# Seven products in all three feed-forward stages, state-space parameters split over two of them, and streamed half tiles at odd multiples of 64 bytes

## The chip, the cores and the metric

The kernel runs on one core of a Trainium2 chip. A core has TensorE (PE in the rows, with its weight loads as PEld), VectorE (DVE), ScalarE (ACT), GpSimd (POOL), and SyncE (SP), which here issues all the DMAs. The metric is the device time of one execution in microseconds, less is better.

## The reference

Two layers of a first block, then one layer of a second block, on 512 tokens of width 1024, all in float32:

```python
# hybrid_layer, twice
h = rms_norm(x, g_mix_pre); u = h @ w_in
# band attention, a causal convolution and a retention on slices of u
mix = concatenate([y_att, y_conv, y_ret]) @ w_out
x = x + rms_norm(mix, g_mix_post)
h = rms_norm(x, g_mlp_pre)
f = square(relu(h @ w_up)) @ w_down            # 1024 -> 4096 -> 1024
x = x + rms_norm(f, g_mlp_post)

# second_block, once
proj = rmsnorm(h, norm1_gain) @ w_in           # q, k, v, u, gates
# differential attention on q, k, v
# s5_layer on u: lambda = exp((a_re + i a_im) * exp(log_dt)), a scan over time with it
h = h + (g_attn * attn_branch + g_ssm * ssm_branch) @ w_out
up = causal_dwconv(rmsnorm(h, norm2_gain) @ w_up)
gate, val = split(up)                          # 2816 each
h = h + (silu(gate) * val) @ w_down
```

The state-space part needs powers of lambda and tables of its cosines and sines. They depend on parameters alone, not on x.

## The kernel before

**Products.** Each float32 operand is split in two fp32r tiles, `hi` (rounded, by ACT's cast) and `lo` (the rest, by a subtraction), and each product is made as hi·hi + hi·lo + lo·hi: three matmuls (`mm3`). Weights stream in from HBM as `wraw` tiles of 128x1024 and are split to `whi`/`wlo` by class `Stream`. Normalized activations lie transposed in `hhi`/`hlo` (128 x 8 x 512). In a row's name the streamed (moving) operand comes first, then the stationary one: `ps<-hhi,whi` streams `hhi` against weights `whi`; `ps<-whi,fhi` streams weights against the activations `fhi`.

**Stages, in order.** Hybrid layer 0, its MLP (called MLP 0 here, rows from 261.9 us), hybrid layer 1, its MLP (MLP 1, from 888.6 us), the second block's mixer, and its feed-forward (FF 2, from 1742.4 us). An MLP has a head (`f_split`: four 128-wide chunks of `w_up`, done in two halves of 256 tokens), a body (the other 28 chunks and seven of eight groups of `w_down`) and a tail (the last group of `w_down`, the norms, and the transposes `to_hT` for what comes next).

**Seven products.** `FAST = (1,)` names the layers whose MLP takes two chunks of `w_up` at a time with seven products in place of eight (Strassen's scheme in Winograd's form): `take_fast` (line 808) makes sums of weight tiles (`wsum`), `fast_in` (1135) makes sums of activations (`sraw`, then `shi`/`slo`), and `FastUp` runs 7 x 4 x 3 = 84 matmuls of 256 columns for two chunks, with `mid` and `cu` as intermediates. Without it, two chunks are 2 x 8 x 3 = 48 matmuls of 512 columns. MLP 1 (`mlp`, 1708) has 14 such pairs and FF 2 (`ffn2`) has 20. MLP 0 (`mlp_plain`, 1649) has none.

**State-space parameters.** `ssm_params` (1802) is a side task of MLP 0. It makes small 128x32 values (`prm`) on DVE and ACT, eight `combine` results on POOL (`t<-sbc,prm`), and eight pairs of tables on POOL (`t<-t,prm` and `t<-t`, 42 operations a pair), each closed by one DVE multiply (`t<-t,pv`) and two DMAs. Each `yield 3000` puts the due time of what follows 3000 ns later.

**Order.** The program records all instructions (`Trace`) and a list scheduler gives them their order from due times and estimated costs, and an engine where two can do it: `sub` and `sum` go to DVE or POOL by a bias, chosen by `self.wbias` (3 favours POOL, 1 excludes it; 3 in `mlp_plain`, 1 in `mlp` and `ffn2`, 2 in the hybrid layers). Each engine then runs its queue in that order. An instruction may stand up to 25.16 us ahead of its due time. SBUF tiles of 128x512 come from one pool, `sp`, with 58 places.

**Addresses.** In the program before, every fp32r operand that is streamed through TensorE starts at a multiple of 256 bytes in its partition.

Of the kernel before, what the change touches and what calls it, by code (L numbers as in the profile page):

```python
# [17 lines left out]
P = 128  # L18
S = 512
# [27 lines left out]
NF2 = DFF2 // 128  # L47
FAST = (1,)

# [887 lines left out]
class Builder:  # L937
# [11 lines left out]
    def __init__(self, tc, ctx, A, out):  # L949
        self.tc, self.nc, self.A, self.out = tc, Trace(tc.nc), A, out  # L950

        def pool(name, bufs, shape=None, dtype=F32, space="SB"):
            kw = {} if space == "SB" else {"space": bass.MemoryType.PSUM if space == "PS" else bass.MemoryType.DRAM}
            return Pool(lambda n: ctx.enter_context(tc.tile_pool(name=n, bufs=1, **kw)), name, bufs, shape, dtype, space)
        self.cp = pool("cp", None)
        self.wr = pool("wr", self.NR, [P, 1024])
        self.wh, self.wl = pool("wh", self.NW, [P, 1024], F32R), pool("wl", self.NW, [P, 1024], F32R)
        self.sp = pool("sp", 86 - 2 * self.NR - 4 * self.NW, [P, 512])
        self.stp = pool("stp", 16, [P, 32])
        self.jp = pool("jp", 2, [P, 512], BF16)  # L960
        self.psp = pool("psp", 4, [P, 512], F32, "PS")
        self.pss = pool("pss", 4, [P, 512], F32, "PS")
        self.dp = pool("dp", None, space="DRAM")
        self.side = Side(self)
        self.T = 30000.0
        self.in_side = False
        self.wbias = 2
        self.rawT = None
        self.before = None
        self.seven = False  # L970
# [164 lines left out]
    def fast_in(self):  # L1135

        nc, R = self.nc, self.rawT
        self.rawT = None
        S = {}
        for j in range(2):  # L1140
            s1, s2, s4, s3 = (self.s2(name="sraw") for _ in range(4))
            nc.sub(s1, R[1, j], R[1, j + 2], self.wbias)
            nc.sub(s2, s1, R[0, j], self.wbias)
            nc.sum(s4, R[0, j + 2], s2, self.wbias)
            nc.sub(s3, R[0, j], R[1, j], self.wbias)
            for i, s in ((6, s2), (5, s1), (3, s4)):
                hi, lo = self.s2(F32R, "shi"), self.s2(F32R, "slo")
                nc.copy(hi, s)
                nc.sub(lo, s, hi.bitcast(F32), self.wbias)
                S[i, j] = [z.rearrange("p (k n) -> p k n", k=2) for z in (hi, lo)]  # L1150
            hi, lo = (z[:, 2 * j:2 * j + 2, 256:512] for z in (self.hhi, self.hlo))
            v = s3.rearrange("p (k n) -> p k n", k=2)
            nc.copy(hi, v)
            nc.sub(lo, v, hi.bitcast(F32), self.wbias)

        def a(i, k):
            if i == 1:
                return self.hT(k, 0, 256)
# [19 lines left out]
    def fast_end(self, steps=(4, 3)):  # L1178
        if self.before:
            for i in steps:  # L1180
                self.before.run(i)
            if 3 in steps:
                self.before = None

    def run(self):
        nc, tc, A = self.nc, self.tc, self.A
        self.pvt = self.cp.tile(F32, "pv", [P, PV_N])
        self.cm = self.cp.tile(F32, "cm", [P, 4 * P])
        self.rope = self.cp.tile(F32, "rope", [P, NT, 64])
        self.hhi = self.cp.tile(F32R, "hhi", [P, KD, S])  # L1190
        self.hlo = self.cp.tile(F32R, "hlo", [P, KD, S])
        self.mhalf = self.cp.tile(F32, "mhalf", [P, 32])
# [14 lines left out]
        nc.vector.memset(self.ones.bitcast(F32), 1.0)  # L1207
        nc.vector.memset(self.epsc, EPS)
        self.prio(-8000.0)
        load_x(0)  # L1210
# [322 lines left out]
    def hybrid(self, l):  # L1533
# [10 lines left out]
        for t in range(NT):  # L1544
            z = self.s2(name="rtab")
            nc.sync.dma_start(out=z[:, :RT_N], in_=A["rtab"][t])
            tabs.append(z)
# [26 lines left out]
        def rot(w):  # L1574
            def f(t, ps):
                d = self.s2(name="rqk")
                self.ret_rot(t, ps, w, tabs[t], d)
# [42 lines left out]
        self.side.drain()  # L1620
        self.rawT = {} if l in FAST else None
        self.finish(lambda t: (p0[t],), 4, W_OUT_KS, mix, X, gpost, gpre)
        self.mix = {}
# [25 lines left out]
    def mlp_plain(self, l, X):  # L1649
        nc = self.nc  # L1650
        groups = mlp_groups()
        self.wbias = 3
        if l == 0:
            self.side.add(self.ssm_params())
        acc = [None] * NT
# [52 lines left out]
    def mlp(self, l, X):  # L1708
        nc = self.nc
        self.wbias = 1  # L1710
        self.seven = True
        xm = self.spill(X, f"xm{l}")
        del X
# [64 lines left out]
    def finish_mlp(self, f, acc, xm, gpost, gpre, store):  # L1778
        nc = self.nc
        ks = sorted(f)  # L1780
        lhs = lambda k, t0, t1: tuple(z[:, t0:t1] for z in f[k])
# [20 lines left out]
    def ssm_params(self):  # L1802
# [36 lines left out]
        ang = mul(aim, dt)  # L1839
        yield 3000  # L1840
        k = x
# [9 lines left out]
        si, co = new(), new()  # L1851
        yield 3000
        nc.scalar.activation(si, r, AF.Sin)
        V.scalar_tensor_tensor(co, r, -1.0, r, op0=ALU.mult, op1=ALU.max)
        V.tensor_scalar(co, co, -1.0, math.pi / 2, op0=ALU.mult, op1=ALU.add)
        nc.scalar.activation(co, co, AF.Sin)
        yield 3000
        lb = (mul(mag, co), mul(mag, si))
# [6 lines left out]
        V.reciprocal(den, den)  # L1865
        yield 3000
        cr, ci = new(), new()
# [7 lines left out]
        mul(s1, den, ci)  # L1875
        yield 3000
        ms = k
# [28 lines left out]
        for t in range(4):  # L1906
            V.tensor_scalar(q, d[1], nsg[:, 0:1], None, op0=ALU.mult)
            combine(d[0], q, sb[0], sb[1], self.gd[3 - t])
            yield 3000
            if t < 3:  # L1910
                d = cmul(d, lb, d)
                yield 3000
        ee = (d[0], d[1])
# [3 lines left out]
        for t in range(4):  # L1917
            V.tensor_scalar(q, ee[0], sgn, None, op0=ALU.mult)
            V.tensor_scalar(q2, ee[1], -1.0, None, op0=ALU.mult)
            combine(q, q2, sb[2], sb[3], self.hd[t])  # L1920
            yield 3000
            if t < 3:
                ee = cmul(ee, lb, ee)
                yield 3000
        del sb
# [3 lines left out]
        for j in range(7):  # L1929
            if j:  # L1930
                ph = cmul(ph, ph)
            pw.append(ph)
            yield 3000
        self.ctd = [self.dp.tile(F32, f"ctd{i}", [P, 512]) for i in range(8)]
        self.std = [self.dp.tile(F32, f"std{i}", [P, 512]) for i in range(8)]
        for b in range(8):
# [4 lines left out]
            for j in range(7):  # L1941
# [11 lines left out]
                if j > 3:  # L1953
                    yield 3000
            V.tensor_scalar(Sn, Sn, sgn, None, op0=ALU.mult)
            nc.sync.dma_start(out=self.ctd[b], in_=C)
            nc.sync.dma_start(out=self.std[b], in_=Sn)
            yield 3000

# [86 lines left out]
    def dq_evac(self, p, t, ps, cg, sg):  # L2046
# [7 lines left out]
        nc.vector.tensor_scalar(self.rq[:, p, :, t], st[:, 8:12], 0.125, None, op0=ALU.mult)  # L2054
        a, b, d = self.s2(), self.s2(), self.s2(name="dqk")
        v4 = lambda z: z.rearrange("p (a g d) -> p a g d", a=2, d=64)
# [73 lines left out]
    def second(self):  # L2130
# [13 lines left out]
        self.subl = st[:, 6:7]  # L2144
        self.mask = self.s2(name="mask")
        nc.gpsimd.memset(self.mask[:, :384], 0.0)
        nc.gpsimd.tensor_copy(self.mask[:, 384:], self.tri)
        self.rq = self.cp.tile(F32, "rq", [P, 4, 4, NT])
        cg, sg = self.s2(name="cg"), self.s2(name="sg")
        go = PV["gqk"][0]  # L2150
# [119 lines left out]
        hs = {}  # L2270
        self.rawT = {}
        for t in range(NT):
            ps = self.ps()
# [56 lines left out]
def hybrid_stack_kernel(ctx: ExitStack, tc, A, out):  # L2330
    b = Builder(tc, ctx, A, out)
    b.run()
    order = b.nc.order()
    for t in (b.mhalf, b.hhi, b.hlo):
        t.place()
# [20 lines left out]
```

## Time and profile before

| | us |
|---|---|
| three runs | 2103.12, 2100.49, 2101.51; median 2101.51 |
| the profiled execution | 2105.0, its span 2103.3 |
| PE busy in the span | 2015.8 (96%), 11188 matmul records |
| DVE, ACT, POOL busy | 1527.6 (73%), 1042.0 (50%), 691.8 (33%) |
| granted TensorE clock, mean | 0.988 |

Stretches are given in us from the span's start. PE is pipelined: a matmul's own duration in a row overlaps its neighbours', so the pace is read from starts or from counts in a stretch. The profile was taken from one execution; the runs are others of the same kernel.

### The profile page before, as it was taken

How to read it: one execution, taken by the hardware profiler on the slowest of the kernel's cores; microseconds unless marked ns; L12 is line 12 of the kernel's file. 1: busy time of each engine (PE TensorE's matmuls, PEld its weight loads, DVE VectorE, ACT ScalarE, POOL GpSimd, SP SyncE). 2: the span in 40 equal slices, each digit the busy share in tenths (PEclk: the TensorE clock that was granted, in tenths of full speed). 3: DMA queues.
4: the chain of work that ended last, by engine and by line, in shares of the span. 5: the costliest groups of instructions: out<-in, count | busy, mean ns of one | idle time of the engine just before them, and what ended most of it. 6: DMA issues, size and time to landing. Idle time of an engine off the chain costs nothing. (4 is left out here: it accounts for less than half of the span.)

```text
span 2103.3 us, 29992 instructions
## 1 busy us (share of the span) xinstructions
PE 2015.8 (96%) x11188; PEld 1745.7 (83%) x11188; DVE 1527.6 (73%) x2485; ACT 1042.0 (50%) x1773; POOL 691.8 (33%) x846
## 2 busy tenths in 40 slices
PE   7999889999999999999999999999999999999999
PEld 7987788778888987799988987677777889989998
DVE  5999695344457999576776773678688649889887
ACT  3378434222233388564444444366477326545543
POOL 4662357960014662200000037763753430000000
PEclk9999989999999999999999999999999999999999
DMA  5423334333242423332423564232425521333322
GB/s 191 133 61 120 122 105 129 112 110 100 80 126 91 133 62 121 98 91 81 132 89 101 180 197 125 71 96 60 120 65 156 163 87 61 101 101 101 121 79 92
DMA packets 87873, 229.53 MB, mean 109 GB/s; under 512 B 10672, under 2 KB 20656, under 8 KB 87728
## 3 DMA queue, kind: packets, MB, share of 16 engines
q1 hardware_dynamic: 87728, 227.62, 34.4%
q8 instruction: 88, 1.44, 0.3%
q14 instruction: 57, 0.47, 0.1%
HBM read 206.35 MB, written 21.23 MB: 108 GB/s over the span
## 5 line engine op out<-in xcount | busy, mean ns | idle before, releaser
L674 ACT CAST whi<-wraw 128x1024 fp32r<-128x1024 f32 (+1 forms) x324 | 332.0, 1031 | 448.2 <-PE ps L674 373.6
L674 POOL TENSOR_TENSOR wlo<-wraw,whi 128x1024 fp32r<-128x1024 f32 (+1 forms) x144 | 337.1, 2347 | 526.3 <-ACT whi L674 433.6
L674 PE MATMUL ps<-hhi,whi 128*128 128x256 f32 (+1 forms) x1488 | 454.9, 331 | 7.2 <-ACT hhi L674 2.3
L674 PE MATMUL ps<-hlo,whi 128*128 128x256 f32 (+1 forms) x1488 | 452.3, 329 | 9.6 <-DVE hlo L674 9.6
L674 PE MATMUL ps<-hhi,wlo 128*128 128x256 f32 (+1 forms) x1488 | 449.8, 328 | 1.2 <-DVE wlo L674 1.2
L674 PEld LDWEIGHTS ps<-hlo,whi 128*128 128x128 f32 x1488 | 273.1, 194 | 34.1 <-DVE hlo L674 10.9
L674 PEld LDWEIGHTS ps<-hhi,whi 128*128 128x128 f32 x1488 | 273.4, 194 | 33.5 <-ACT hhi L674 3.3
L674 PEld LDWEIGHTS ps<-hhi,wlo 128*128 128x128 f32 x1488 | 271.9, 193 | 24.2 <-DVE wlo L674 1.4
L674 DVE TENSOR_TENSOR wlo<-wraw,whi 128x1024 fp32r<-128x1024 f32 x190 | 235.8, 1247 | 59.7 <-ACT whi L674 59.5
L674 PE MATMUL ps<-whi,fhi 128*128 128x512 f32 x688 | 251.0, 392 | 7.5 <-DVE t L674 4.4
L674 PE MATMUL ps<-wlo,fhi 128*128 128x512 f32 x688 | 251.9, 392 | 1.6 <-DVE wlo L674 1.6
L674 PE MATMUL ps<-whi,flo 128*128 128x512 f32 x688 | 252.4, 392 | 0.0
L674 DVE TENSOR_TENSOR acc<-ps,acc 128x512 f32<-128x512 f32 x112 | 76.1, 687 | 122.9 <-PE ps L674 122.8
L674 PE MATMUL ps<-whi,hhi 128*128 128x384 f32 (+1 forms) x448 | 154.5, 370 | 5.2 <-DVE vlo L674 3.5
L674 PE MATMUL ps<-wlo,hhi 128*128 128x384 f32 (+1 forms) x448 | 154.9, 369 | 1.2 <-POOL wlo L674 1.2
L674 PEld LDWEIGHTS ps<-whi,fhi 128*128 128x128 f32 x688 | 129.1, 188 | 31.4 <-DVE t L674 4.8
L674 PE MATMUL ps<-whi,hlo 128*128 128x384 f32 (+1 forms) x448 | 153.7, 369 | 0.0
L674 PEld LDWEIGHTS ps<-wlo,fhi 128*128 128x128 f32 x688 | 129.8, 189 | 26.6 <-DVE wlo L674 2.9
L674 PEld LDWEIGHTS ps<-whi,flo 128*128 128x128 f32 x688 | 129.7, 189 | 24.3
L674 PE MATMUL ps<-shi,whi 128*128 128x256 f32 (+1 forms) x440 | 124.3, 292 | 0.6 <-ACT mid L674 0.6
L674 PE MATMUL ps<-slo,whi 128*128 128x256 f32 (+1 forms) x440 | 124.2, 291 | 0.0
L674 PE MATMUL ps<-shi,wlo 128*128 128x256 f32 (+1 forms) x440 | 124.0, 290 | 0.0
(272 smaller groups left out, 3896.8 us busy)
## 6 DMA issues: line engine op xcount, KB each, us to landing
wraw<-in_wst SPq DMA_DIRECT2D x302, 512.0 KB, 3.7
wraw<-in_wst SPq DMA_DIRECT2D x32, 384.0 KB, 3.1
gain<-in_gains SPq DMA_DIRECT2D x20, 256.0 KB, 4.7
X<-in_x SPq DMA_DIRECT2D x16, 256.0 KB, 5.2
xd<-X SPq DMA_DIRECT2D x16, 256.0 KB, 2.4
X<-xd SPq DMA_DIRECT2D x16, 256.0 KB, 6.1
gated<-t SPq DMA_DIRECT2D x16, 256.0 KB, 3.0
gate<-gated SPq DMA_DIRECT2D x16, 256.0 KB, 4.2
```

Source lines behind the costliest of these rows:

```text
L674: getattr(getattr(self.nc, e), m)(*[r(x) for x in op.args], **{k: r(v) for k, v in op.kw.items()})
```

## The change

`FAST` becomes `(0, 1)`, so that MLP 0 runs `mlp` too, with `wbias` 1. The side task is cut in two: `ssm_params` (all up to the powers `pw`) goes to MLP 0 and `ssm_tables` (the eight pairs of tables) to MLP 1, each put in 30 us after the stage's start and with wider steps. `hhi` and `hlo` get 32 more columns and are used 16 columns (64 bytes) further on from the end of the hybrid layer or mixer to the MLP's tail, so that their 256-column halves start at odd multiples of 64 bytes. A pool `sq` of 12 tiles stands behind a 64-byte pad; `shi`/`slo` come from it in the feed-forward stages, and in the others some tiles that came from `sp` (`rtab`, `rqk`, `dqk`, `mask`, `cg`, `sg`). `sp` has 46 places in place of 58. Matmuls of 256 columns that start at an odd multiple of 64 bytes: 1368 in MLP 0 (192 of the head, 14 x 84 of the body), as many in MLP 1, and 1872 in FF 2 (192 and 20 x 84), 4608 in all.

```diff
-FAST = (1,)
+FAST = (0, 1)
...
-        self.sp = pool("sp", 86 - 2 * self.NR - 4 * self.NW, [P, 512])
+        self.sp = pool("sp", 74 - 2 * self.NR - 4 * self.NW, [P, 512])
...
+        self.pad = pool("pad", 1, [P, 16])
+        self.sq = pool("sq", 12, [P, 512])
...
-                hi, lo = self.s2(F32R, "shi"), self.s2(F32R, "slo")
+                hi, lo = self.sq.tile(F32R, "shi"), self.sq.tile(F32R, "slo")
...
+    def shift(self, n):
+
+        self.hhi, self.hlo = (z[:, n:n + KD * S].rearrange("p (k n) -> p k n", k=KD) for z in self.hbig)
...
-        self.hhi = self.cp.tile(F32R, "hhi", [P, KD, S])
-        self.hlo = self.cp.tile(F32R, "hlo", [P, KD, S])
+        self.hbig = [self.cp.tile(F32R, n, [P, KD * S + 32]) for n in ("hhi", "hlo")]
+        self.shift(0)
...
         self.rawT = {} if l in FAST else None
+        self.shift(16 if l in FAST else 0)
         self.finish(lambda t: (p0[t],), 4, W_OUT_KS, mix, X, gpost, gpre)
...
-        if l == 0:
-            self.side.add(self.ssm_params())
...
         self.wbias = 1
         self.seven = True
+        self.side.add((self.ssm_params, self.ssm_tables)[l](), 30000)
...
     def finish_mlp(self, f, acc, xm, gpost, gpre, store):
         nc = self.nc
+        self.shift(0)
...
-        yield 3000
+        yield 7000
...
+        self.pw = pw
+
+    def ssm_tables(self):
...
-                    yield 3000
+                    yield 8000
...
         self.rawT = {}
+        self.shift(16)
```

POOL's queue in MLP 0, before, at the end of a pair of tables (`prm` are powers, `t` the tables, `wlo` the low half of a streamed weight tile):

```order
L674 TENSOR_TENSOR t<-t,prm_3771 128x4x32
L674 TENSOR_TENSOR t<-t,prm_3817 128x4x64
L674 TENSOR_TENSOR t<-t 128x4x32
L674 TENSOR_TENSOR t<-t,prm_3650 128x4x2
L674 TENSOR_TENSOR t<-t,prm_3820 128x4x64
...
L674 TENSOR_TENSOR t<-t,prm_3820 128x4x64
L674 TENSOR_TENSOR wlo<-wraw,whi 128x1024
L674 TENSOR_TENSOR t<-t 128x4x64
```

The same engine with the change, from hybrid layer 0's end into MLP 0:

```order
L674 TENSOR_TENSOR wlo<-wraw,whi 128x1024 x8
L674 TENSOR_TENSOR st<-st,mhalf 128x1 x8
L674 TENSOR_TENSOR t<-sbc,prm_3733 128x512
L674 TENSOR_TENSOR t<-sbc,prm_3750 128x512
L674 TENSOR_TENSOR t<-t 128x512
```

There MLP 0 has no tables on POOL any more, and three `wlo` where there were eleven; the tables stand in MLP 1, where POOL has no `wlo`.

DVE's queue around the multiply that closes a pair of tables (`t<-t,pv`), in MLP 0 before:

```order
L674 MEMSET t 128x4 x2
L674 TENSOR_SCALAR t<-ps 128x512
L674 TENSOR_TENSOR wlo<-wraw,whi 128x1024
L674 TENSOR_TENSOR flo<-t,fhi 128x512
L674 TENSOR_TENSOR acc<-ps,acc 128x512
L674 TENSOR_SCALAR t<-t,pv 128x512
L674 TENSOR_TENSOR acc<-ps,acc 128x512 x2
```

and in MLP 1 with the change:

```order
L674 TENSOR_TENSOR flo<-cu,fhi 128x512
L674 TENSOR_TENSOR wlo<-wraw,whi 128x1024
L674 TENSOR_TENSOR flo<-cu,fhi 128x512
L674 TENSOR_TENSOR acc<-ps,acc 128x512
L674 TENSOR_TENSOR wlo<-wsum,whi 128x512
...
L674 TENSOR_TENSOR acc<-ps,acc 128x512 x2
L674 TENSOR_SCALAR t<-t,pv 128x512
L674 TENSOR_TENSOR acc<-ps,acc 128x512
L674 TENSOR_TENSOR cu<-ps,mid 128x256
```

The multiply stands between the same kinds of work in both. Between the last POOL operation of its pair of tables and the multiply the program before places 1 to 77 matmuls (six of the eight times at most 18); with the change it places 72 to 251.

TensorE's queue in FF 2, and those of DVE, ACT, POOL and SP there, hold the same instructions in the same order in both programs; only addresses differ. In MLP 0 TensorE's queue goes from `hhi,whi 128x512` triples to the form that MLP 1 has.

## Rows read from the trace of the kernel before

**Rows 1.** The page: engines' busy time, and the chain that ended last.

```profile
PE 2015.8 (96%) x11188; PEld 1745.7 (83%) x11188; DVE 1527.6 (73%) x2485; ACT 1042.0 (50%) x1773; POOL 691.8 (33%) x846
...
PE 21%; DVE 3%; ACT 1%; issue 0%; DVEq 0%
```

**Rows 2.** Busy time of each engine in MLP 0, MLP 1 and FF 2.

```profile
core 0: us, PE busy (x) PEld busy (x) DVE busy (x) ACT busy (x) POOL busy (x), PEclk, DMA share, GB/s
261.90:641.40 379.50, 361.97 (x1664) 302.20 (x1665) 208.17 (x340) 123.79 (x172) 175.32 (x375) 0.97 0.35 107
888.60:1241.90 353.30, 347.55 (x2176) 314.40 (x2177) 252.60 (x378) 170.62 (x283) 14.62 (x14) 0.99 0.38 120
1742.40:2103.30 360.90, 351.22 (x2417) 324.88 (x2416) 310.09 (x451) 189.09 (x298) 0.93 (x1) 1.00 0.29 94
```

**Rows 3.** The same, by pieces: MLP 0, hybrid 1, MLP 1, mixer.

```profile
261.90:299.30 37.40, 30.98 (x215) 29.70 (x216) 34.22 (x67) 13.27 (x23) 21.57 (x19) 0.83 0.29 94
...
365.00:445.00 80.00, 70.54 (x296) 56.91 (x295) 28.33 (x45) 15.71 (x19) 77.96 (x221) 0.96 0.32 106
445.00:594.00 149.00, 149.00 (x657) 123.34 (x656) 74.98 (x82) 48.46 (x59) 19.25 (x18) 1.00 0.35 103
594.00:641.40 47.40, 45.76 (x210) 37.81 (x210) 28.30 (x40) 17.55 (x33) 8.82 (x7) 1.00 0.32 106
641.40:888.60 247.20, 236.70 (x1304) 210.10 (x1302) 201.56 (x353) 140.12 (x269) 112.14 (x132) 0.99 0.33 102
888.60:917.40 28.80, 26.60 (x208) 26.40 (x209) 26.46 (x44) 18.94 (x41) 2.03 (x3) 0.94 0.28 91
917.40:1192.70 275.30, 275.29 (x1764) 250.60 (x1763) 191.59 (x276) 130.84 (x202) 0.68 (x2) 1.00 0.35 109
1192.70:1241.90 49.20, 45.66 (x208) 37.40 (x207) 34.55 (x59) 20.83 (x41) 11.91 (x9) 0.95 0.59 195
1241.90:1742.40 500.50, 479.62 (x2314) 381.85 (x2312) 339.37 (x579) 269.97 (x474) 261.63 (x184) 0.98 0.36 109
```

**Rows 4.** PE in order of time, MLP 1's body: 256-column matmuls (start, us).

```profile
1164.82 0.28 PE L674 MATMUL ps<-shi,whi 128*128 128x256 f32 x1
...
1165.30 0.28 PE L674 MATMUL ps<-hhi,wlo 128*128 128x256 f32 x1
...
1165.78 0.29 PE L674 MATMUL ps<-hhi,whi 128*128 128x256 f32 x1
```

**Rows 5.** PE in order of time: eight transposes, 128 columns each, on end.

```profile
659.94 1.04 PE L674 MATMUL ps<-cm,t 128*128 128x128 f32 x8
```

**Rows 6.** DVE in order of time in MLP 0: head, then two closing multiplies.

```profile
263.75 3.14 DVE L674 TENSOR_TENSOR X<-X,t 128x512 f32<-128x512 f32 x2
...
375.18 0.50 DVE L674 TENSOR_SCALAR t<-t,pv 128x512 f32<-128x512 f32 x1 [7.78 <-POOL t L674]
...
390.32 0.56 DVE L674 TENSOR_SCALAR t<-t,pv 128x512 f32<-128x512 f32 x1 [9.92 <-POOL t L674]
```

**Rows 7.** POOL and PE in order of time, MLP 0: beside those waits.

```profile
263.40 2.34 POOL L674 TENSOR_TENSOR wlo<-wraw,whi 128x1024 fp32r<-128x1024 f32 x1 [1.04 <-ACT whi L674]
...
391.53 0.79 PE L674 MATMUL ps<-whi,fhi 128*128 128x512 f32 x1 [4.40 <-DVE t L674]
```

**Rows 8.** Groups of DVE, MLP 0 (two rows), then MLP 1 (two rows).

```profile
L674 DVE TENSOR_TENSOR wlo<-wraw,whi 128x1024 fp32r<-128x1024 f32 x52 | 67.5, 1301 | 14.9 <-ACT whi L674 14.6
...
L674 DVE TENSOR_TENSOR flo<-t,fhi 128x512 fp32r<-128x512 f32 x32 | 29.2, 912 | 4.7 <-ACT t L674 4.5
...
L674 DVE TENSOR_TENSOR wlo<-wraw,whi 128x1024 fp32r<-128x1024 f32 x63 | 76.5, 1223 | 12.9 <-ACT whi L674 12.9
...
L674 DVE TENSOR_TENSOR flo<-cu,fhi 128x512 fp32r<-128x512 f32 x32 | 21.9, 687 | 1.3 <-ACT cu L674 0.8
```

**Rows 9.** Busy time on tile `prm` (DVE, ACT, POOL), then `t` (all engines).

```profile
261.90:641.40 379.50, 23.79 (x105) 0.00 (x0) 96.11 (x238) 0.97 0.35 107
...
324.00:456.00 132.00, 0.00 (x0) 0.00 (x0) 21.04 (x42) 11.39 (x18) 117.57 (x336) 0.97 0.34 109
```

More of the change, by code (lines that the diff above doesn't have):

```diff
@@ L1208, in run @@
         nc.vector.memset(self.epsc, EPS)
+        nc.vector.memset(self.pad.tile(name="pad"), 0.0)
         self.prio(-8000.0)
@@ L1544, in hybrid @@
         for t in range(NT):
-            z = self.s2(name="rtab")
+            z = self.sq.tile(name="rtab")
             nc.sync.dma_start(out=z[:, :RT_N], in_=A["rtab"][t])
@@ L1575, in f @@
             def f(t, ps):
-                d = self.s2(name="rqk")
+                d = self.sq.tile(name="rqk")
                 self.ret_rot(t, ps, w, tabs[t], d)
@@ L1851, in ssm_params @@
         si, co = new(), new()
-        yield 3000
+        yield 7000
         nc.scalar.activation(si, r, AF.Sin)
@@ L1856, in ssm_params @@
         nc.scalar.activation(co, co, AF.Sin)
-        yield 3000
+        yield 7000
         lb = (mul(mag, co), mul(mag, si))
@@ L1865, in ssm_params @@
         V.reciprocal(den, den)
-        yield 3000
+        yield 7000
         cr, ci = new(), new()
@@ L1875, in ssm_params @@
         mul(s1, den, ci)
-        yield 3000
+        yield 7000
         ms = k
@@ L1908, in ssm_params @@
             combine(d[0], q, sb[0], sb[1], self.gd[3 - t])
-            yield 3000
+            yield 7000
             if t < 3:
                 d = cmul(d, lb, d)
-                yield 3000
+                yield 7000
         ee = (d[0], d[1])
@@ L1920, in ssm_params @@
             combine(q, q2, sb[2], sb[3], self.hd[t])
-            yield 3000
+            yield 7000
             if t < 3:
                 ee = cmul(ee, lb, ee)
-                yield 3000
+                yield 7000
         del sb
@@ L1932, in ssm_params @@
             pw.append(ph)
-            yield 3000
+            yield 7000
+        self.pw = pw
+    def ssm_tables(self):
+        nc, V, pw = self.nc, self.nc.vector, self.pw
+        o, w = PV["sgn"]
+        sgn = self.pvt[:, o:o + w]
         self.ctd = [self.dp.tile(F32, f"ctd{i}", [P, 512]) for i in range(8)]
@@ L1953, in ssm_params @@
                 if j > 3:
-                    yield 3000
+                    yield 8000
             V.tensor_scalar(Sn, Sn, sgn, None, op0=ALU.mult)
@@ L1957, in ssm_params @@
             nc.sync.dma_start(out=self.std[b], in_=Sn)
-            yield 3000
+            yield 8000
     def ssm_task(self, us, ud, yd):
@@ L2054, in dq_evac @@
         nc.vector.tensor_scalar(self.rq[:, p, :, t], st[:, 8:12], 0.125, None, op0=ALU.mult)
-        a, b, d = self.s2(), self.s2(), self.s2(name="dqk")
+        a, b, d = self.s2(), self.s2(), self.sq.tile(name="dqk")
         v4 = lambda z: z.rearrange("p (a g d) -> p a g d", a=2, d=64)
@@ L2144, in second @@
         self.subl = st[:, 6:7]
-        self.mask = self.s2(name="mask")
+        self.mask = self.sq.tile(name="mask")
         nc.gpsimd.memset(self.mask[:, :384], 0.0)
@@ L2148, in second @@
         self.rq = self.cp.tile(F32, "rq", [P, 4, 4, NT])
-        cg, sg = self.s2(name="cg"), self.s2(name="sg")
+        cg, sg = self.sq.tile(name="cg"), self.sq.tile(name="sg")
         go = PV["gqk"][0]
@@ L2333, in hybrid_stack_kernel @@
     order = b.nc.order()
-    for t in (b.mhalf, b.hhi, b.hlo):
+    for t in [b.mhalf] + b.hbig:
         t.place()
```

## The prediction

> **What bounds the kernel now.** I read the page's engine totals first. PE is busy for 96% of the span, and the chain that ended last is PE work wherever its rows name an engine for long [rows 1]. So the time is the sum of PE's stages, and the question in each is how far PE's own pace and its idle stretches can shrink. The view by stage [rows 2] shows three feed-forward stages of about 350 to 380 us each. MLP 0 and MLP 1 compute the same thing on the same shapes, MLP 0 plainly and MLP 1 with seven products: 379.5 us against 353.3 us. That pair is the best row there is for the main edit, since MLP 0 becomes the code of MLP 1.
>
> The pieces [rows 3] show where the 26.2 us lie. The head takes 37.4 us in MLP 0 and 28.8 in MLP 1. The body takes 294.7 us (594.0 - 299.3) against 275.3. The tail takes 47.4 against 49.2. In MLP 0's body the stretch from 365 to 445 us has PE busy for only 70.5 of 80 us, while POOL is busy for 78.0: the tables of the state-space part fill POOL. DVE, which runs its queue in order, stands behind the multiplies that close a pair of tables, 7.8 and 9.9 us in the two rows shown, and PE waits for DVE's next product 4.4 us after the second [rows 6, 7].
>
> PE's pace: in MLP 0's undisturbed body 657 matmuls of 512 columns take 149.0 us, 226.8 ns each [rows 3]. In MLP 1's body eight steps between 256-column matmuls take 0.96 us, 120 ns each, whether `hhi` or `shi` is streamed [rows 4]. The extra 256 columns cost 106.8 ns, so a matmul costs its columns plus some 13 ns that do not depend on width. This is why seven products gain less than an eighth: two chunks cost 48 x 226.8 = 10.89 us plainly and 84 x 120 = 10.08 us with seven products.
>
> **The change, part by part.**
>
> *Seven products in MLP 0.* 14 pairs save 14 x 0.81 = 11.3 us of PE time. The measured body difference is 19.4 us, the head's is 8.6 and the tail's is -1.8, together **-26.2 us**. I take the measured difference of the whole stages, because it also holds what 256- and 512-column work costs when mixed, the spill and reload of X (16 more DMAs of 256 KB on SP, DMA share 0.38 in MLP 1), and the end of the stalls at the tables. The head's part has a reason in the rows: in MLP 0 a pair of additions `X<-X,t` on DVE takes 3.14 us while POOL holds a 2.34 us `wlo` [rows 6, 7], and the clock is granted at 0.83 in that head against 0.94 in MLP 1's [rows 3]. With `wbias` 1 the first `wlo` of the stage go to DVE, as in MLP 1. The bounds: 11.3 us if the stalls come back in another form, 28 if the tail does not pay its 1.8.
>
> *`ssm_params` stays in MLP 0.* Its small DVE operations take 23.8 us in that stage [rows 9], and some ran before it. MLP 1's form has DVE busy for 252.6 of 353.3 us; 252.6 + 24 is 78%, and FF 2 runs at 310.1 of 360.9, 86%, with PE busy for 351.2 [rows 2]. So DVE has cover and I cost this at 0. If the cover went, the price would be at most its own 24 us. ACT (170.6 of 353.3) covers its four activations.
>
> *`ssm_tables` in MLP 1.* POOL works 117.6 us for the 336 table operations [rows 9], in a stage where it is otherwise free, busy for 14.6 us [rows 2]. What can hurt is DVE. First, the closing multiply: the order now puts 72 to 251 matmuls between the last table operation and the multiply, 8.6 us of matmuls or more at 120 ns, so the waits of 7.8 and 9.9 us should be gone. Second, the two engines slow each other: with tables on POOL `wlo` takes 1301 ns where it takes 1223 in MLP 1, and `flo` 912 where it takes 687 [rows 8]. That is 52 x 0.078 + 32 x 0.225 = 11.3 us of DVE time; over MLP 1's larger number of such operations I allow 20. 252.6 + 20 + eight multiplies is 78% again, covered. I take **+1 us**.
>
> [...] If each microsecond of the tables shut DVE out, DVE would need 252.6 + 117.6 + 4 = 374 us for MLP 1, 21 us over its 353.3; this is the third rival.
>
> *The pools.* 12 of `sp`'s 58 places become `sq`. In the feed-forward stages `sq` holds the same 12 tiles that `sp` held. In the hybrid layers and the mixer the order changes somewhat. PE idles 10.5 us of 247.2 in hybrid 1 and 20.9 of 500.5 in the mixer [rows 3]; the order may win or lose a few of these. I take 0, with 4 us to either side.
>
> *Odd starts.* 1368 + 1368 + 1872 = 4608 matmuls start at an odd multiple of 64 bytes, which no matmul of this trace does. The nearest rows are the 256-column matmuls at even starts: 120 ns for every operand. The lower end is set by the weight loads: eight 128-column transposes on end take 1.04 us with 0.27 us for the last one's own length, (1.04 - 0.27)/7 = 110 ns each [rows 5], although they stream only 128 columns, so a matmul with a load of its own does not go faster. So at best 10 ns each, 46 us. The other end: if the odd start costs a second time the fixed 13 ns, 60 us more. Between them I take 0, as the even rows are nearest and do not depend on the operand; but the fixed part is paid per matmul and not per column, which is where a start address would act, so the gain keeps a large chance. FF 2 is the place to see it: all its queues are the same as before.
>
> [...]
>
> *Sum.* -26.2 + 1 = -25.2 us. The profiled execution took 2105.0 us, 3.5 above the median 2101.5, so 2079.8 by its own time and **2076 us** against the median, in its own range 2066 to 2086.
>
> **The rivals.**
>
> *Odd starts gain.* The fixed part of 13 ns shrinks, to the weight loads' 110 ns at best. For: it is the same at both widths, so it sits at the start. Against: nothing shows that address matters. MLP 0 and MLP 1 would give 2 x 1368 x 10 = 27 us. FF 2 would give up to 19 us, but DVE is at 86% there and would be at 91%, so I count 14. With all of it 2076 - 41 = 2035 us, with half of it 2056. [...]
>
> *The stalls come back.* The side work meets DVE's queue in another place, and only the columns are saved: 2101.5 - 11.3 = 2090 us. For: DVE has over 20 us more to do in MLP 0 than MLP 1 had. Against: FF 2 at 86%.
>
> *DVE shut out by the tables.* As worked out, MLP 1 takes 374 us: 2076 + 21 = 2097 us. Against it stand the 11 us [rows 8].
>
> *Odd starts cost.* This one ends on the other side. Each of 4608 matmuls pays a further fixed part because its stream begins inside a piece that must be fetched whole: at 13 ns each 60 us, 2076 + 60 = 2136 us. It decides from 25.2 us / 4608 = 5.5 ns on; below that the kernel stays faster. Nothing in the rows speaks for it, and no row has such a start.
>
> **How the numbers follow.** Forecast 0.47, odd starts gain 0.33, stalls come back 0.08, DVE shut out 0.05, odd starts cost 0.07. About 0.2% (4 us) is what a measurement of this kernel can tell from no change. Faster: 0.47 + 0.33 + 0.08 and half of the 0.05, 0.90. Same: the rest of that and a little of the costly case, 0.04. Slower: 0.06. The range reaches from 2032, a little beyond the full gain, to 2092, beyond the returning stalls; outside it lie the last two cases and a trifle below, some 0.13.
>
> **What would show it.** MLP 0 at 353 us, with a head near 29 us and no PE idle stretch in its body; no `t<-t,pv` that waits for POOL for microseconds; MLP 1 at 353 to 356 us with POOL some 130 us busy in it, `flo` there near 0.8 us. FF 2 within 2 us of 360.9 and its 256-column matmuls at 120 ns say that odd starts do nothing; 110 to 116 ns say that they gain, and FF 2 ends 11 to 19 us sooner; 126 or more make the forecast wrong. So does an MLP 0 over 368 us.

## The result, and the profile of the changed kernel

The changed kernel takes 2139.9 us (median; 2136.4 to 2141.9) where the kernel before took 2101.6 beside it: **slower, by a ratio of 1.0177 (95% interval 1.0162 to 1.0191)**. The prediction said 2076 us, in 2032 to 2092, and faster.

The first view is again busy time by stage. These are the changed kernel's six stages, cut where [rows 2] and [rows 3] cut those of before (each begins with the first product of `hhi` with `whi`; the columns are those of [rows 2]): hybrid 0, MLP 0, hybrid 1, MLP 1, mixer, FF 2.

```profile
0.00:289.90 289.90, 251.35 (x1318) 218.91 (x1318) 207.31 (x357) 148.04 (x280) 119.96 (x138) 0.96 0.33 107
289.90:639.10 349.20, 343.49 (x2169) 310.75 (x2170) 273.22 (x502) 169.44 (x282) 44.92 (x36) 0.99 0.38 124
639.10:917.30 278.20, 249.68 (x1303) 216.27 (x1301) 209.03 (x358) 138.50 (x266) 110.76 (x133) 0.94 0.28 88
917.30:1272.30 355.00, 346.21 (x2177) 312.57 (x2177) 262.63 (x400) 168.92 (x280) 153.97 (x348) 0.99 0.40 131
1272.30:1781.30 509.00, 484.63 (x2314) 387.16 (x2312) 341.00 (x581) 270.49 (x476) 260.43 (x183) 0.97 0.34 108
1781.30:2138.50 357.20, 346.89 (x2417) 321.08 (x2416) 309.25 (x451) 189.30 (x298) 0.93 (x1) 1.00 0.28 95
```

Hybrid 0 of the kernel before, which [rows 3] do not hold:

```profile
0.00:261.90 261.90, 238.79 (x1318) 212.32 (x1318) 215.77 (x389) 148.40 (x282) 127.20 (x143) 1.00 0.39 125
```

Against [rows 2, 3]: MLP 0 379.5 to 349.2 us, MLP 1 353.3 to 355.0, FF 2 360.9 to 357.2. Together these three gained 32.3 us. Hybrid 0 went from 261.9 to 289.9, hybrid 1 from 247.2 to 278.2, the mixer from 500.5 to 509.0: 67.5 us lost. The difference, 35.2 us, is that of the two spans (2138.5 and 2103.3). The three feed-forward stages, for which the edits were made, did as forecast; the three others lost twice as much.

The rows say how, too. Hybrid 0 runs 1318 matmuls in both kernels; PE is busy 12.6 us longer for them (251.35 and 238.79) at a granted clock of 0.96 in place of 1.00, and idle for 15.4 us more. The next view is a stretch of hybrid 0 in which retention and attention run as side work, 140 to 210 us: first before, then after.

```profile
140.00:210.00 70.00, 66.50 (x334) 54.86 (x332) 65.97 (x136) 54.07 (x103) 23.19 (x21) 1.00 0.32 106
```

```profile
140.00:210.00 70.00, 50.84 (x216) 39.99 (x215) 46.12 (x80) 39.75 (x72) 21.77 (x35) 0.86 0.21 68
```

PE, DVE and ACT are all less busy, PE with 216 matmuls in place of 334. No engine has become the limit; each stands idle for another. PE in order of time shows on what (the bracket is idle time and what ended it):

```profile
141.19 0.60 PE L674 MATMUL ps<-cm,rqk 128*128 128x128 f32 x4
147.93 0.77 PE L674 MATMUL o<-pthi,vhl 128*128 128x512 f32 x1 [6.14 <-DVE ptlo L674]
148.50 0.63 PE L674 MATMUL o<-ptlo,vhl 128*128 128x512 f32 x1
148.92 0.52 PE L674 MATMUL o<-pthi,vhl 128*128 128x384 f32 x1
...
198.59 0.43 PE L674 MATMUL ps<-khi,stk 128*128 128x512 f32 x1
204.33 1.94 PE L674 MATMUL ps<-cm,row 128*128 128x128 f32 x8 [5.31 <-DVE row L674]
```

At 198.59 PE makes the last scores of an attention head; ACT's exponentials and DVE's scaling of its rows follow, and the transposes of these rows come 5.31 us later with nothing in between. The view of PE's waits, hybrid 0 (us in total, times, longest), the rows on tiles of retention and attention, after and then before:

```profile
PE o L674 <- DVE ptlo L674: 8.4, 4, 6.1
PE ps L674 <- DVE row L674: 7.8, 3, 5.3
...
PE ps L674 <- DVE ptlo L674: 3.6, 2, 3.4
```

```profile
...
PE ps L674 <- DVE row L674: 3.9, 4, 1.6
PE o L674 <- DVE ptlo L674: 2.5, 2, 1.4
```

The same kinds of tiles are waited for, 1.6 us at most before and 6.1 now. My reading is that before, a second chain of side work filled the wait; e1 below, where this stretch is full again, fits it. And with more idle time came a lower granted clock, 0.86 in this stretch where it was 1.00 before. Two 10 us slices of the changed kernel:

```profile
140.00:150.00 10.00, 3.85 (x17) 3.15 (x15) 4.56 (x8) 5.65 (x8) 5.51 (x9) 0.80 0.33 105
...
200.00:210.00 10.00, 5.04 (x19) 4.43 (x20) 5.65 (x15) 4.45 (x13) 0.00 (x0) 0.70 0.35 115
```

In the first slice, which holds the 6.14 us without a matmul, the granted clock is 0.80: 1.00 from 140.00 to 141.79 us, 0.84 over the wait, 0.50 from 147.93 to 150.00. After the wait the 512-column matmul at 148.50 is followed by the next 0.42 us later, where such a step took 0.23 before at a granted 1.00 (142.56 to 142.79 us). In the second, 5.31 us without a matmul at 0.97 are followed by 0.50 from 204.33 to 210.00. By PE's busy time, 251.35 us against 238.79, I estimate the clock's part at some 12.6 of hybrid 0's 28.0 us.

### The profile page after: what moved, and what is told of

It reads as the page before. It is cut to its first block, busy times and chain, and to the rows that moved or that the text cites. A ratio compares the mean times of both kernels' runs of the same rounds, so it can differ in the third digit from the quotient of the medians.

```text
span 2138.5 us, 31383 instructions
## 1 busy us (share of the span) xinstructions
PE 2022.2 (95%) x11692; PEld 1766.7 (83%) x11692; DVE 1602.5 (75%) x2644; ACT 1084.7 (51%) x1877; POOL 691.0 (32%) x836
## 5 line engine op out<-in xcount | busy, mean ns | idle before, releaser
L674 POOL TENSOR_TENSOR wlo<-wraw,whi 128x1024 fp32r<-128x1024 f32 (+1 forms) x134 | 308.7, 2310 | 612.1 <-ACT whi L674 499.2
L674 ACT CAST whi<-wraw 128x1024 fp32r<-128x1024 f32 (+1 forms) x317 | 324.5, 1030 | 257.1 <-PE ps L674 190.4
L674 PE MATMUL ps<-hlo,whi 128*128 128x256 f32 (+1 forms) x1488 | 423.1, 311 | 8.2 <-DVE hlo L674 8.2
L674 PE MATMUL ps<-hhi,whi 128*128 128x256 f32 (+1 forms) x1488 | 424.9, 313 | 4.9 <-ACT hhi L674 2.3
L674 PE MATMUL ps<-hhi,wlo 128*128 128x256 f32 (+1 forms) x1488 | 421.7, 311 | 1.3 <-DVE wlo L674 1.3
L674 DVE TENSOR_TENSOR wlo<-wraw,whi 128x1024 fp32r<-128x1024 f32 x200 | 248.8, 1252 | 56.7 <-ACT whi L674 56.6
L674 PE MATMUL ps<-shi,whi 128*128 128x256 f32 (+1 forms) x608 | 168.6, 289 | 3.6 <-DVE cu L674 2.1
L674 PE MATMUL ps<-slo,whi 128*128 128x256 f32 (+1 forms) x608 | 167.4, 287 | 0.0
L674 PE MATMUL ps<-shi,wlo 128*128 128x256 f32 (+1 forms) x608 | 167.3, 286 | 0.0
L674 ACT COPY mid<-ps 128x256 f32<-128x256 f32 x144 | 52.9, 368 | 224.1 <-PE ps L674 224.1
```

The costliest lines, as they stand in the source:

```text
L674: getattr(getattr(self.nc, e), m)(*[r(x) for x in op.args], **{k: r(v) for k, v in op.kw.items()})
```

## The experiments

The theory after this: the loss is the split of `sp` into 46 and 12 places. The scheduler starts an instruction only when each new tile finds a free place in its own pool (`room`); with fewer places it puts fewer chains of side work beside each other. Rival A: not the pool, but what else moved (seven products in MLP 0, the parameters) changed due times and order. Two smaller questions: what odd starts do, and why the tables did no harm in MLP 1. In us, stages of each profiled execution cut as above, medians of the timed runs (hybrid 0 counts from 0 here; the expectations count it from PE's first matmul, 7 us later):

| kernel | H 0 | MLP 0 | H 1 | MLP 1 | mixer | FF 2 | median |
|---|---|---|---|---|---|---|---|
| before | 261.9 | 379.5 | 247.2 | 353.3 | 500.5 | 360.9 | 2101.6 |
| the change | 289.9 | 349.2 | 278.2 | 355.0 | 509.0 | 357.2 | 2139.9 |
| e1 one pool | 259.7 | 349.6 | 244.9 | 354.7 | 502.3 | 359.1 | 2072.6 |
| e2 one pool, all odd | 260.9 | 348.8 | 247.0 | 354.9 | 505.2 | 361.0 | 2079.0 |
| e3 before, split | 292.6 | 377.6 | 278.6 | 351.9 | 502.1 | 360.6 | 2167.9 |
| e4 change, even | 291.5 | 349.9 | 281.6 | 355.3 | 505.4 | 358.8 | 2141.8 |
| e5 one pool, even | 259.9 | 351.1 | 245.4 | 355.5 | 501.4 | 361.2 | 2076.8 |
| e6 one pool, 256 spare | 259.8 | 350.1 | 244.6 | 355.4 | 500.2 | 358.5 | 2071.4 |
| e7 one pool, tables in MLP 0 | 260.2 | 399.4 | 245.8 | 351.0 | 500.1 | 358.5 | 2116.7 |
| e8 before, 52 places | 290.7 | 379.7 | 275.6 | 353.3 | 505.9 | 360.7 | 2166.8 |
| e9 one pool, steps of 3 us | 259.7 | 359.9 | 244.8 | 382.5 | 501.7 | 358.5 | 2107.9 |
| e10 change, 12 places empty | 300.6 | 349.2 | 288.7 | 356.4 | 501.1 | 357.4 | 2154.6 |
| e11 before, 56 places | 267.1 | 380.3 | 248.1 | 352.3 | 503.2 | 360.7 | 2113.9 |
| e12 e6 with 56, fifth `wr` | 264.3 | 353.5 | 248.5 | 358.4 | 501.8 | 350.2 | 2077.7 |

### The pool

**e1**, the change with its pool whole:

```diff
-        self.sp = pool("sp", 74 - 2 * self.NR - 4 * self.NW, [P, 512])
+        self.sp = pool("sp", 86 - 2 * self.NR - 4 * self.NW, [P, 512])
-        self.pad = pool("pad", 1, [P, 16])
-        self.sq = pool("sq", 12, [P, 512])
+        self.sq = self.sp
```

> The change with its 58 places in one pool again (shi and slo back in it and so at even starts; hhi and hlo keep their odd starts). Theory: the loss is the split of the pool, 28 us in hybrid 0, 31 in hybrid 1 and 9 in the mixer, 68 in all, so 2140 - 68 = 2072 us, and 2076 with the 4 us that shi and slo lose without odd starts; hybrid 0 at 255, hybrid 1 at 247, the mixer at 500. Rival A (seven products in MLP 0 and the moved parameters change the due times and with them the order in the hybrid layers, whatever the pool): 2130 to 2145 us, hybrid layers at 280. Rival B (the odd starts of sq cost in the layers that read rqk and rtab): 2072 too, but then the run with 58 odd places is slow.

Measured 2072.6 us, ratio to before 0.9857 (0.9842 to 0.9872). Hybrid 0 and 1 are at 259.7 and 244.9, and the stretch of 140 to 210 us reads as before the change:

```profile
140.00:210.00 70.00, 66.98 (x335) 55.11 (x333) 65.93 (x136) 54.27 (x103) 23.18 (x21) 1.00 0.31 106
```

Between the two profiled executions lie 68.2 us; hybrid 0 has 30.2 of them, hybrid 1 33.3, the mixer 6.7. Rival A falls.

**e3**, the other way round: the kernel before with only the split.

```diff
-        self.sp = pool("sp", 86 - 2 * self.NR - 4 * self.NW, [P, 512])
+        self.sp = pool("sp", 74 - 2 * self.NR - 4 * self.NW, [P, 512])
+        self.sq = pool("sq", 12, [P, 512])
-            z = self.s2(name="rtab")
+            z = self.sq.tile(name="rtab")
...
```

> The kernel before with nothing but the pool split into 46 and 12 places (even starts, no seven products in MLP 0, parameters where they were). Theory: hybrid 0 +28, hybrid 1 +31, mixer +9, so 2101.5 + 68 = 2170 us, all of it in these three stages. Rival A (the loss comes from the moved work, not from the pool): 2101 us within 6.

Measured 2167.9 us, ratio 1.0309 (1.0294 to 1.0324). Hybrid 0 and hybrid 1:

```profile
0.00:292.60 292.60, 252.43 (x1318) 220.16 (x1318) 214.87 (x391) 148.91 (x281) 128.38 (x143) 0.96 0.35 112
...
670.20:948.80 278.60, 248.39 (x1303) 215.21 (x1301) 210.83 (x357) 138.70 (x266) 111.92 (x132) 0.94 0.28 90
```

30.7 and 31.4 us more than before, so the split alone does it in these two layers. The mixer's part did not come as expected: 502.1, 1.6 more, not 9.

Is it the number of places, or that `rtab` and `rqk` may use only the 12 (rival D)? **e8** takes 6 places from the one pool of the kernel before (86 to 80 in the line of `sp`), **e10** takes `rtab` and `rqk` from the 46 and leaves the 12 empty in the hybrid layers, **e11** takes 2 places (86 to 84).

> The kernel before with 52 in place of 58 places in its one pool, nothing else. Theory (what counts is how many places the hybrid layers' side work finds free): both hybrid layers lose, 30 to 70 us in all, so 2132 to 2172 us, and the feed-forward stages nothing. Rival D (58 places are more than is needed, and what hurt in the split is that rtab and rqk may use the 12 places of their own pool only): 2102 to 2110 us.

> The change, with rtab and rqk taken from the pool of 46 instead of the pool of 12, so that these 12 places stand empty in both hybrid layers. Theory (the number of places that the layer can use counts): the hybrid layers take 5 to 25 us more each than the 281 and 276.5 of the change, 2150 to 2190 us, the mixer as in the change. Rival D (tiles bound to the small pool were what waited): hybrid layers back to 255 to 265 us, 2090 to 2115 us.

> The kernel before with 56 in place of 58 places in its one pool. Six places fewer cost 62.7 us. If each place has its price (10.4 us), two cost 21: 2125 us, half in each hybrid layer. If there is an edge (the hybrid layers need some number of places between 52 and 56, and nothing above it), two cost under 5: 2101 to 2108 us. Theory as it stands does not choose; I lean to the edge, as the split with 46 and 12 places cost no more than 52 in one pool.

e8: 2166.8 us, ratio 1.0291 (1.0275 to 1.0307), 28.8 and 28.4 us in the hybrid layers, 5.4 in the mixer. Nothing is tied to a small pool there. Its stretch of 140 to 210 us is that of the change:

```profile
140.00:210.00 70.00, 52.31 (x220) 41.14 (x221) 51.52 (x83) 39.58 (x75) 22.88 (x41) 0.83 0.28 87
```

e10: 2154.6 us, ratio 1.0245 (1.0230 to 1.0260); the hybrid layers take 10.7 and 10.5 us more than in the change. Rival D asked for the opposite. (The mixer was expected as in the change and took 501.1 us in place of 509.0; see "Open" below.) e11: 2113.9 us, ratio 1.0053 (1.0040 to 1.0065), some 11 us for two places, 5.2 in hybrid 0, 0.9 in hybrid 1 and 2.7 in the mixer. That lies between its two expectations, and I had leaned to the wrong one, the edge: the first two places already cost 5 us each, the next four 13 each (62.8 us for six). Where between 56 and 52 places the cost rises was not tried. Against this scale 46 and 12 places are worth no more than 52 in one pool. A reading of the code fits, though no run shows it by itself: an attention head in flight holds three `row` tiles and six of `pthi` and `ptlo`, so a dozen places are about one head.

### The starts

**e2** puts the 64-byte pad ahead of one pool of 58, so that all its tiles start odd; **e4** takes the pad and `shift(16)` out of the change; **e5** takes `shift(16)` and the 128 spare bytes behind `hhi` and `hlo` out of e1; **e6** makes these spare bytes 256.

```diff
+        self.pad = pool("pad", 1, [P, 16])
         self.sp = pool("sp", 86 - 2 * self.NR - 4 * self.NW, [P, 512])
```

```diff
-        self.shift(16 if l in FAST else 0)
+        self.shift(0)
```

```diff
-        self.hbig = [self.cp.tile(F32R, n, [P, KD * S + 32]) for n in ("hhi", "hlo")]
+        self.hbig = [self.cp.tile(F32R, n, [P, KD * S + 64]) for n in ("hhi", "hlo")]
```

> The change with one pool of 58 places, all of them behind the 64-byte pad, so that every tile in it starts at an odd multiple of 64 bytes, in all stages. Theory: same order as the run with one pool, and 2 ns less for each matmul that streams one of its tiles: 2072 us for the three feed-forward stages alone, down to 2060 if the matmuls of the hybrid layers, the mixer and the down products that stream such tiles gain 2 ns each too. Rival A: 2130 to 2145 us. Rival B (odd starts cost outside the feed-forward stages): 2085 us or more, with hybrid layers over 260 us.

> The change with even starts everywhere: hhi and hlo not moved, no pad ahead of the 12 places; the order of the instructions is the same. Theory: 4608 matmuls take 120 in place of 118 ns, 9 us more, so 2149 us, FF 2 at 357 in place of 353. Rival C (odd starts are worth nothing, FF 2's 3.7 us have another cause): 2140 us within 3, 118 ns stay. If odd starts were a cost somewhere else: under 2140 us.

> The run with one pool, and hhi and hlo neither moved nor given spare bytes: seven products in MLP 0 and the divided parameters alone. The order of the instructions is that of the run with one pool. Theory: the 256-column matmuls go back from 118.2 to 119.65 ns, 4608 x 1.4 = 6.5 us lost, and the 512-column ones outside the feed-forward stages from 229.8 to 228.2 ns, some 3 us gained: 2072.6 + 3.5 = 2076 us. Rival (the placement is worth nothing in sum): 2072 us within 1.5.

> The run with one pool, with 256 in place of 128 spare bytes behind hhi and behind hlo, so that both start at the same place modulo 256 bytes (odd multiples of 64 in the feed-forward stages as before). Theory E (it is hlo's 128 bytes against hhi that slows the 512-column matmuls of hybrid layers and mixer from 228.2 to 229.8 ns): these go back, the mixer takes 500 to 501 in place of 503.4 us, and the whole 2069 us if the 256-column ones stay at 118.2. Rival (the 118 ns came from the same 128 bytes and not from the odd start): 256-column matmuls at 119.5 and the whole 2073 to 2077.

FF 2 shows the pace best. In each of the kernels the same piece of it holds 149 matmuls of 256 columns on end, 148 steps from the first start to the last. Busy time by stretch, that piece, in before, the change, e4, e5 and e6:

```profile
1828.11:1845.85 17.74, 17.74 (x149) 17.73 (x148) 17.21 (x26) 11.89 (x19) 0.00 (x0) 1.00 0.30 87
```

```profile
1866.20:1883.64 17.44, 17.44 (x149) 17.44 (x148) 17.04 (x25) 11.94 (x19) 0.00 (x0) 1.00 0.28 86
```

```profile
1869.06:1886.57 17.51, 17.51 (x150) 17.50 (x148) 17.09 (x25) 11.92 (x19) 0.00 (x0) 1.00 0.27 86
```

```profile
1798.97:1816.71 17.74, 17.74 (x150) 17.74 (x148) 17.20 (x26) 11.88 (x19) 0.00 (x0) 1.00 0.31 91
```

```profile
1794.73:1812.23 17.50, 17.50 (x150) 17.50 (x148) 17.04 (x25) 11.90 (x19) 0.00 (x0) 1.00 0.28 88
```

Divided by 148, a step takes 119.9 ns before, 117.8 in the change, 118.3 in e4, 119.9 in e5, 118.2 in e6 (a count over the edge of a stretch is 150). So the address does matter, by 1.6 to 2 ns, and there are two ways to nearly the same gain. e6 has `hhi` and `hlo` at odd multiples of 64 bytes and the same place modulo 256 (`shi` and `slo` even): 1.6 ns over the mix of them. e4 has no odd start at all, but `hlo` lies 128 bytes off `hhi`'s place modulo 256: 1.6 ns as well, which I had put down to odd starts. That is why e4 lost so little: 2141.8 us, ratio 1.0184 (1.0169 to 1.0199), not to be told from the change's, where 2149 was expected. The numbers are those of rival C, and for most of the gain it was right that no odd start is needed. The mean step between any two 256-column matmuls of FF 2 whose starts lie under 135 ns apart, at a granted clock of 1.00, is 119.7, 118.5 and 117.6 ns for before, e4 and the change, so the odd starts add 0.9 there. The same mean by streamed operand shows more: in e6 the steps of `hhi` and `hlo` take 117.0 to 117.2 ns, those of the even `shi` and `slo` 118.8 to 119.8, where before all take 119.7. So an odd start is worth some 2.6 ns there to the matmul that has it.

The 128 bytes have a price elsewhere: between 512-column matmuls of the mixer the same kind of mean is 227.9 ns before, 229.9 in the change, 227.7 in e6, whose mixer is back at 500.2 us. By operand most of it is at `hlo`, the tile that is 128 bytes off: steps that stream it take 227.9 ns before and 233.3 in the change, steps that hold it as weights 228.9 and 233.2. Theory E of e6 holds, and its rival, which wanted 119.5 ns, falls. In whole times these are small: e5 came where its theory had it, 2076.8 us, 0.9870 (0.9857 to 0.9884), e6 0.9848 (0.9835 to 0.9862) of before, intervals that touch. FF 2 shows it (361.2 and 358.5); the whole hardly does.

e2 missed: 2079.0 us, ratio 0.9884 (0.9867 to 0.9900), 6 us more than e1 where up to 12 less had been hoped for, and its hybrid layers (260.9, which is some 254 as the expectation counts, and 247.0) exclude a rival B of the size given. In MLP 1's tail, 151 matmuls of 512 columns with `fhi` or `flo` held in PE as weights, in the change and then in e2:

```profile
1224.64:1258.68 34.04, 34.04 (x152) 28.16 (x151) 21.11 (x41) 11.86 (x23) 3.52 (x3) 1.00 0.51 169
```

```profile
1165.37:1200.37 35.00, 35.00 (x152) 28.06 (x151) 21.40 (x41) 11.72 (x23) 3.52 (x3) 1.00 0.50 170
```

227 ns a step in the first, 233 in the second. The stream (`whi`, `wlo` from their own pools) starts even in both; what e2 moved is the operand that is loaded as weights. An odd start there costs 6 ns.

### The tables

**e7** leaves e1's parameters undivided in MLP 0, from its start and in the old steps; **e9** keeps them divided, in the old steps.

```diff
-        self.side.add((self.ssm_params, self.ssm_tables)[l](), 30000)
+        if l == 0:
+            self.side.add(self.ssm_all())
...
-            yield 7000
+            yield 3000
...
-                    yield 8000
+                    yield 3000
```

(e9 has the `yield` lines alone.)

> The run with one pool, with the parameter work undivided: all of it in MLP 0, from its start and in steps of 3 us as in the kernel before, while MLP 0 has its seven products. Theory (the tables slow VectorE's operations and their closing multiply holds its queue, and VectorE is nearer its limit in this form): MLP 0 takes 5 to 20 us more than 351, MLP 1 1 to 2 less than 355: 2075 to 2090 us. Rival (the division buys nothing, the tables are covered in MLP 0 as well): 2071 to 2073 us.

> The run with one pool, parameters divided as in the change, but in the old steps of 3 us instead of 7 and 8 us. Undividing them and setting these steps together cost 44 us, nearly all in MLP 0, where VectorE's closing multiply of the tables waited 39.8 us for GpSimd and PE waited 28.7 us for cu behind it. Theory F (the steps set how soon the multiply's turn comes on VectorE's queue; they did it): MLP 1 takes 20 to 50 us more than 355, the whole 2095 to 2120 us. Rival G (the division did it: tables alone in MLP 1 leave VectorE enough room whatever the steps): 2072 us within 4.

e7: 2116.7 us, ratio 1.0063 (1.0051 to 1.0076). MLP 0 takes 399.4, 50 more than in e1 and beyond the 5 to 20 expected. The view of waits in MLP 0, PE's and then DVE's:

```profile
PE ps L674 <- DVE cu L674: 28.7, 4, 15.3
...
DVE t L674 <- POOL t L674: 39.8, 8, 9.3
```

All eight closing multiplies stand at the head of DVE's queue while POOL finishes, 39.8 us in sum, and PE waits for the `cu` queued on DVE; and from 300 to 340 us DVE is full (39.56 of 40 us), 27.1 of it with `prm`:

```profile
300.00:340.00 40.00, 27.19 (x153) 23.47 (x151) 39.56 (x105) 13.91 (x22) 27.59 (x25) 0.90 0.23 77
```

e9: 2107.9 us, ratio 1.0020 (1.0011 to 1.0029). MLP 1 takes 382.5 and MLP 0 359.9, 27.8 and 10.3 more than in e1. DVE in order of time, MLP 1 of e9 and then of the change:

```profile
928.64 0.51 DVE L674 TENSOR_SCALAR t<-t,pv 128x512 f32<-128x512 f32 x1 [8.11 <-POOL t L674]
...
982.54 0.59 DVE L674 TENSOR_SCALAR t<-t,pv 128x512 f32<-128x512 f32 x1 [6.99 <-POOL t L674]
```

```profile
995.81 0.48 DVE L674 TENSOR_SCALAR t<-t,pv 128x512 f32<-128x512 f32 x1
...
1058.83 0.49 DVE L674 TENSOR_SCALAR t<-t,pv 128x512 f32<-128x512 f32 x1 [2.61 <-POOL t L674]
```

In sum the eight multiplies of e9 wait 34.2 us for POOL, those of the change 3.3. So theory F has its number: of the 44 us between e7 and e1, the longer steps are worth 35. The other 9 belong to the division together with the later start, which e7 took back too; undivided work in the longer steps was not tried.

The way that theory F names, how soon the multiply's turn comes, is not borne out. By the count of the section on the change, e9's order places 16 to 246 matmuls between the last table operation and the multiply, six of the eight times 153 or more; with the change it is 72 to 251 (and before it six of the eight are at most 26, not 18). The multiply shown at 949.79 below has 157 of them ahead of it and still waits. What the steps changed is how densely POOL works. That multiply, then POOL's busy time on the tables in e9 and in the change:

```profile
949.79 0.53 DVE L674 TENSOR_SCALAR t<-t,pv 128x512 f32<-128x512 f32 x1 [6.29 <-POOL t L674]
```

```profile
890.00:1032.00 142.00, 0.00 (x0) 0.00 (x0) 4.50 (x22) 0.00 (x0) 121.53 (x294) 0.92 0.30 105
```

```profile
930.00:1200.00 270.00, 1.28 (x8) 0.83 (x8) 4.67 (x23) 0.00 (x0) 130.50 (x305) 0.99 0.34 109
```

POOL is busy with tables for 121.5 of 142 us in e9 and for 130.5 of 270 in the change. A POOL that is nearly full falls behind its place in the order, and DVE's multiply waits wherever it stands; that reading fits the rows, no run shows it by itself.

### A fifth buffer of raw weights

**e12** is e6 with `NR` 5 in place of 4, which leaves `sp` 56 places.

> The fastest so far (one pool, 256 spare bytes, 2071.4 us) with two places of the pool given up for a fifth buffer of raw weights. If there is an edge below 56 places: 2055 to 2072 us, since weights can be loaded earlier. If each place has its price: 2085 us or more, with hybrid layers over 260 us.

2077.7 us, ratio 0.9879 (0.9863 to 0.9895). FF 2 gains 8.3 us on e6 (350.2), but both hybrid layers lose 4 each and the MLPs 3 each: neither expectation held, and in sum it loses 6 us. The best versions are e6 and e1, 2071.4 and 2072.6 us, which cannot be told apart.

## Why the prediction was wrong

**The step that failed is "The pools": "I take 0, with 4 us to either side".** Restoring the one pool gives back 67 us (2139.9 and 2072.6); the split alone costs 65 (2167.9 and 2103.1, before in that comparison), 62 of them in the two hybrid layers. I had priced it by PE's idle time, 10.5 us in hybrid 1 and 20.9 in the mixer. That is the bound of what a better order can win. What a worse order can lose has no bound in those rows: it had to be read from how much of the layer runs side by side, the 66.5, 66.0 and 54.1 us of PE, DVE and ACT in the same 70 us above, all from chains that wait for each other when alone. And no rival of mine had the pool in it. The odd starts, not the loss of places, took the chance of a slower kernel.

- *Seven products in MLP 0*: right. Forecast 353, measured 349.2; head 30.0 us, body 275.1 without an idle stretch (the row below). With even starts it was 351.1 (e5).

```profile
319.90:595.00 275.10, 275.10 (x1768) 250.05 (x1767) 217.45 (x421) 133.74 (x209) 32.51 (x24) 1.00 0.38 124
```

- *`ssm_params` at 0*: right as measured, but the cover was thin. In steps of 3 us the same work costs MLP 0 10 us (e9), and full DVE is seen in e7.
- *`ssm_tables` at +1*: right in size, 1.7 us against before and 3.7 against the same stage without tables (e1 354.7, e7 351.0). The reason given, that enough matmuls stand ahead of the closing multiply, is not borne out: in six of eight cases e9 has as many, and it loses 27.8 us in MLP 1. What differs is that the longer steps leave POOL half its time. The size came right with a reason that does not carry it, which is luck. One multiply of the change still waits 2.61 us for POOL, where the prediction wanted none that waits for microseconds.
- *DVE shut out by the tables*: excluded. POOL worked 130.50 us on `t` beside MLP 1, and DVE's groups there, which [rows 8] had at 1223 and 687 ns without tables, were:

```profile
L674 DVE TENSOR_TENSOR wlo<-wraw,whi 128x1024 fp32r<-128x1024 f32 x60 | 75.0, 1259 | 10.2 <-ACT whi L674 10.1
...
L674 DVE TENSOR_TENSOR flo<-cu,fhi 128x512 fp32r<-128x512 f32 x32 | 22.0, 690 | 0.8 <-ACT cu L674 0.4
```

  That is 60 x 36 + 32 x 3 ns = 2.3 us. Of DVE's other groups some slowed as well (`wsum<-wsum,wraw` from 685 to 730 ns), `acc<-ps,acc` did not (688 and 685); all together it is some 8 us, an estimate from the groups' means, less than the 11 to 20 that I allowed. That each microsecond of the tables shuts DVE out, no run shows: spread out, their 130.5 us cost DVE some 8.
- *The stalls come back*: not in the change, but this is e7, where they cost 50 us.
- *Odd starts*: 0 was forecast; FF 2 gained 3.7 us at 118 ns, between "120, nothing" and "110 to 116". *Odd starts cost* ends near the measured time, at 2136, by a cost that the 256-column streams do not show (119.9 ns a step before, 117.8 in the change): the time fitted, the cause did not. That a piece is fetched whole, no run shows. A cost of 6 ns, 233 in place of 227, is there for operands loaded as weights (e2), which the change keeps even in the feed-forward stages.

Open: the mixer's 8.5 us in the change. The split alone gives it 1.6 (e3), the 128 spare bytes some 2 (e1 and e6). But neither these, nor the order, nor `dqk` at its odd start make up 8.5: e10 has all of them in the mixer, with every engine's instructions there in the same order, and takes 501.1 us, 0.6 more than before. What differs is the clock. The mixer of e10 (that of the change is in the first view: 509.00 us, PE busy 484.63, clock 0.97):

```profile
1294.95:1796.05 501.10, 477.87 (x2314) 382.24 (x2313) 340.30 (x580) 270.05 (x474) 260.12 (x183) 0.98 0.34 109
```

PE after one and the same wait, in the change and then in e10:

```profile
1368.13 0.79 PE L674 MATMUL ps<-ucm,gt 64*128 64x128 f32 x2 [2.32 <-ACT gt L674]
```

```profile
1389.88 0.48 PE L674 MATMUL ps<-ucm,gt 64*128 64x128 f32 x2 [2.33 <-ACT gt L674]
```

The 10 us that begin there, in the change and then in e10:

```profile
1368.13:1378.13 10.00, 10.00 (x24) 6.11 (x25) 3.44 (x4) 3.47 (x6) 6.21 (x5) 0.50 0.20 61
```

```profile
1389.88:1399.88 10.00, 9.99 (x46) 6.59 (x46) 6.56 (x7) 6.11 (x9) 9.62 (x8) 1.00 0.21 63
```

After the same idle 2.3 us the granted clock is 0.50 in the one execution and 1.00 in the other, and PE's busy time holds 6.8 of the 7.9 us between the two mixers. Why it fell in the one and not in the other, no run shows.

## What to carry to other kernels

When a scheduler fills a stage with side chains, its buffers are its parallelism: here a split pool cost nothing in the feed-forward stages and 30 us a layer where many chains overlap. So price a pool in the stage with the most chains in flight, and from the busy shares of all engines there, not from PE's idle time. Work on a side engine that another engine's in-order queue closes should be spread, by the reading above so that the side engine is not full when the closing operation's turn comes: here longer steps were worth 35 us, more than moving the work to another stage and starting it later (9).

## What the runs showed of the hardware that was not expected

- Streaming 256 columns of fp32r takes 119.9 ns a step in FF 2 with `hhi` and `hlo` at multiples of 256 bytes, and 118.2 to 118.3 with both 64 bytes further (e6) or with `hlo` alone 128 further (e4); with both, and `shi` and `slo` at odd multiples of 64 too, 117.8 (the change).
- For 512-column matmuls of the mixer the 128 bytes cost: those that stream `hlo`, 128 bytes off, take 233.3 in place of 227.9 ns, those that hold it as weights 233.2 in place of 228.9, all together 229.9 in place of 227.9.
- The same wait of PE of 2.3 us, at the same place of the mixer, was followed by 10 us at a granted clock of 0.50 in one execution and of 1.00 in another (the change and e10).
- In MLP 1's tail a 512-column matmul whose weights are loaded from an odd multiple of 64 bytes takes 233 ns a step (e2) in place of 227 (the change).
